# One inference step of a hybrid encoder on one core: the recurrence's normalisers are transposed on chip and stored as whole rows

## The chip, the cores and the metric

The kernel runs on one core of one Trainium2 chip. The metric is the device time of one execution in microseconds (us). Of the kernel before, three runs were timed: 778.81, 780.55 and 783.39 us, median 780.55.

## The reference, cut to what matters

One layer of an encoder is computed for a prompt (1 sequence of 1024 tokens) and for a decode step (8 sequences of 16 new tokens each, so 128 rows as well), all in float32. A normed input of width 1024 goes through one projection, whose columns feed three groups of heads; their gated outputs are joined and go through a second projection.

```python
z = jnp.einsum('bsd,de->bse', rms_norm(x, g_norm), w_in)
# A: 4 heads of differential attention over the new keys, for decode also over 1024 cached ones
# B: 4 heads of an mLSTM, a matrix memory C [64, 64] with a normaliser n [64] for each head
# M: 4 heads of cross-attention into 256 memory tokens
y = x + jnp.einsum('bse,ed->bsd', jnp.concatenate([oa, hb, om], -1), w_out)
```

What matters here is the state of group B. Each chunk of tokens updates it, and the last state is an output, beside `y`, the new keys and values, and others:

```python
C = decay[..., None, None] * C0 + jnp.einsum('bhs,bhsd,bhse->bhde', wS, k, v)
n = decay[..., None] * n0 + jnp.einsum('bhs,bhsd->bhd', wS, k)
```

`C` has the shape [sequence, head, 64, 64] and `n` has [sequence, head, 64]: 4 heads for the prompt, 8 x 4 for the decode step.

## The kernel before, in words

The 1152 rows are cut into 9 tiles of 128 tokens: tiles 0 to 7 are the prompt, tile 8 is the decode step (`DEC`). The normed tiles lie transposed on chip, each split into a high and a low part (`hth`, `htl`), and the weights are split likewise (`wh`, `wl`). A projection of one tile on 512 columns is therefore 24 matmuls of 128 x 512 into one bank of PSUM (`ps_z` or `ps_y`): 8 blocks of the contraction, 3 products each. All matmuls are recorded at line 95, in the helper `mm`.

The work goes through phases: the four heads of A, the gates G, the group M, then two head pairs of B (phases B0 and B1), then the output projection in two halves of columns (O0 and O1). In every phase a weight block is loaded and the tiles pass through it one after the other. `feed` traces the projection of a tile and then one stage more of each tile that is still in the pipeline, so that a tile's later stages lie beside the next tiles' projections. In B0 and B1 a tile of B has three stages: `mlstm_in` (copies out of the bank, two transposes at lines 996 and 997), `mlstm_scores` (loads `mb`, line 1009), and the read-out with the update of the state, which ends in `mlstm_out` (the store of `hb`, line 1042). In phase B0 the decode tile goes first, in B1 third.

Beside B0 and B1 runs the decode attention over the caches, cut into steps by a table: for each of the 8 sequences four loads of keys (`kc`, line 843) and four of values (`vc`, line 875), 512 KB each, in a ring of seven buffers. In O0 the decode attention over the memories follows (`mkc`, line 925, and `mvc`, line 929), two `mkc` buffers; and `out_prep` loads each joined tile (`omx`, line 1136) from a scratch tensor in HBM (`mixd`) for the output projection.

The order in which instructions stand on each engine is not that of the text: a scheduler in the language sets it, by priorities (`ahead`) and by a simulated timeline of its own. All DMAs are issued by SyncE (SP), in one queue and in order; a DMA that must wait for a semaphore holds the ones behind it.

The state of a head pair lies on chip with the head and the row `d` on the 128 partitions. For a decode pair it is `C0` [128, 8 sequences, 65], whose last column is `n`; for the prompt it is `csn` [128, 130], where each head has 65 columns and the last of each 65 is `n`. `C0` has one buffer, so the load of the second pair's state (line 1046) waits until the stores of the first have landed. The stores before: the decode state, 64 columns, at line 1078, and its normaliser, 1 column, at line 1079, once for each pair; the prompt state of each head after the last tile at line 1118 and its normaliser at line 1119. A column that is stored in this way is written as one piece of 4 bytes for each partition and sequence: 1024 pieces for a decode pair, 64 for a prompt head.

Of the kernel before, what the change touches and what calls it, by code (L numbers as in the profile page):

```python
# [11 lines left out]
F32 = mybir.dt.float32  # L12
# [7 lines left out]
P = 128  # L20
# [3 lines left out]
NPT = 8  # L24
# [8 lines left out]
# columns of the relaid w_in: a head of A: q k v ga; ib fb gb; qm gm; a head pair of B: q k v ob  # L33
W_A, W_G, W_M, W_B = 0, 2048, 2312, 2824

# the phases of the projections: priority of the stages before a tile, of its weights and of its
# products; order of the passes for the first tile and the others; banks; engines of the weights' hi
# parts (even k, odd k); k whose lo part is made by Pool; engine that evacuates transposes
# [15 lines left out]
# steps of the decode attention after each tile of the head pairs of B  # L54
# [4 lines left out]
def hymba_step(ctx: ExitStack, tc: tile.TileContext, a: dict, o: dict):  # L59
# [47 lines left out]
    def bc(ap, n):  # L107
        """[p, ...] -> [p, ..., n], repeated along a new last axis"""
        return ap.unsqueeze(len(ap.shape)).broadcast_to(list(ap.shape) + [n])

    def rep(ap, n):
        """[p, ...] -> [p, n, ...], repeated along a new first free axis"""
        return ap.unsqueeze(1).broadcast_to([ap.shape[0], n] + list(ap.shape[1:]))
# [4 lines left out]
    def flat(ap):  # L118
        return ap.rearrange("p a b -> p (a b)")

    # ------------------------------------------------------------------ constants
# [13 lines left out]
    def rsqrt(dst, ss, n):  # L135
        """dst = (ss + n eps) ** -0.5, the reciprocal rms over sqrt(n); the gains carry sqrt(n)"""
        V.tensor_scalar(ss, ss, n * EPS, None, ALU.add)  # L137
        root(dst, ss)
# [15 lines left out]
    # mixed branch outputs and gates of a token tile, stabilisers, values of the new decode tokens  # L154
# [6 lines left out]
    def small_loads():  # L161
# [3 lines left out]
        # carried here: the roots of n, the halves of silu and sigmoid (written with tanh), and, in  # L165
        # the gain of q, 8 * 0.125 / slope of the next head
# [12 lines left out]
    def selectors():  # L179
        # e16[r, q] = (r % 16 == q); bm[r, b] = (r // 16 == b); par[r, i] = ((r // 16) % 2 == i)  # L180
        # h32[r, h] = (r // 32 == h); selc[r, (h, q)] = h32[r, h] * e16[r, q]
# [5 lines left out]
        # sgn[r] = 1 on the rows of map 0, -lam on those of map 1, rows (h, m, q)  # L187
# [6 lines left out]
    def split_T(src, hi, lo, n):  # L194
        """transpose n [128,128] column blocks of src, split into hi and lo [128, n, 128]"""
# [7 lines left out]
    # the tensor engine's clock rises while the first loads run  # L203
# [9 lines left out]
    def weights(w, c0, n, gain=None, spare=()):  # L213
        """columns c0 to c0 + n of a [1024, .] weight, as hi and lo k-tiles; gain scales its rows.
        spare: (pool, tag, bufs) for raw tiles, where there is room"""
# [67 lines left out]
    def norm_T(xt, xp, hi, lo, xT=None):  # L283
        """rms-normed rows (gain not yet applied), transposed and split"""
# [16 lines left out]
    # a token tile's projection is traced ahead of the later stages of the tiles before it  # L301
# [20 lines left out]
    # -------------------------------------------- memory keys and values  # L322
# [9 lines left out]
    # -------------------------------------------- differential attention, prompt  # L332
# [4 lines left out]
    def a_norm(z):  # L337
        """q and k of a head, both maps, over their rms (gains not yet applied)"""
# [16 lines left out]
    def a_post_dec(h, z):  # L355
        """decode tile: q into block-diagonal (m, d) x (b, m, q) stationaries, k transposed"""
# [22 lines left out]
    def a_post(h, t, z, grp):  # L379
        # dist is scaled by the slope, so the scores carry scale / slope  # L380
# [24 lines left out]
        # contraction over (hi, lo) of q in the first map, (lo, hi) in the second  # L405
# [11 lines left out]
    def a_unit(h, t, grp):  # L417
        """attention of one query tile, in two stages"""
# [29 lines left out]
        # the norm takes out the sum of the first map, but for its eps  # L448
# [23 lines left out]
    # -------------------------------------------- mLSTM gate rows: (tile, head) x token in tile  # L472
    R = 36

    def gate_rows():
        # in buffers of the next phase
# [16 lines left out]
        # decode rows restart at every batch  # L493
# [5 lines left out]
        tp = bank("tp")  # L499
# [6 lines left out]
        # log_sigmoid(f) = min(f, 0) - log1p(exp(-|f|)), log1p(u) = 2 atanh(u / (2 + u))  # L506
# [27 lines left out]
        # running stabiliser over the prompt chunks, per head  # L534
# [48 lines left out]
    # -------------------------------------------- cross-attention into the memory  # L583
    def mem_q(z, gt):
        """reciprocal rms of the queries, gate"""
# [10 lines left out]
    def mem_dec_q(z):  # L596
        """decode tile: queries, transposed"""
# [10 lines left out]
    def mem_unit(t, z):  # L608
        # the scores are scaled by the reciprocal rms of q in the softmax; the keys carry q's gain
# [8 lines left out]
        # (hi, lo) of the even heads, (lo, hi) of the odd ones  # L618
# [44 lines left out]
        # this part of the mixed tile stays transposed  # L663
# [43 lines left out]
    # memory keys and values, in buffers that the attention uses later  # L707
    def mem_stages(t):
        def run(z):
# [9 lines left out]
            # 8 of gqm for the 8 that the reciprocal rms of q lacks, times 0.125 of the softmax: none left  # L719
# [63 lines left out]
    # the input and forget gates and gb, behind the last head  # L783
# [27 lines left out]
    # -------------------------------------------- attention over the caches, decode  # L811
    NKD = 1040

    def dec_attention():
# [18 lines left out]
        def scores(b):  # L833
            """rows (h, m, q): exp of the scores over the 1040 keys, signed reciprocal sums"""
# [24 lines left out]
        def values(b, se, sm):  # L859
# [29 lines left out]
            # the two maps, weighted and subtracted: rows (h, q)  # L889
# [21 lines left out]
    # -------------------------------------------- attention over the memories, decode  # L911
    def mem_decode(md):
        """two batches at a time, rows (head, batch of the pair, query)"""
        # contraction over (batch of the pair, head dimension): block-diagonal stationaries
# [48 lines left out]
    # -------------------------------------------- mLSTM  # L963
    # masks over (s, t): prompt causal; decode causal within a batch
# [14 lines left out]
    def mlstm_in(bw, nb, bufs, t, pr, z):  # L979
        """operands of a head pair: values and weighted keys; q (zero-padded), k, gated q transposed"""  # L980
# [24 lines left out]
    def mlstm_scores(bw, nb, t, pr, mask, qk, qp):  # L1005
        """at[s, h, t] = (k_s . q_t) exp(a_s - M_t) on allowed pairs"""
# [11 lines left out]
    def mlstm_out(bw, nb, t, pr, nm, carried, dst, gate):  # L1018
        """read-out, head norm, gates"""
# [13 lines left out]
        # the norm takes out the denominator, but for its eps  # L1033
# [8 lines left out]
        SY.dma_start(out=dst, in_=flat(hb))  # L1042

    def mlstm_decode(pr, z, bufs):
# [24 lines left out]
        for c in range(0, NB, 4):  # L1069
# [9 lines left out]
        SY.dma_start(  # L1079
            out=o["s_n"][0, :, hs].rearrange("b h (d o) -> (h d) b o", o=1), in_=C0[:, :, 64:65]  # L1080
        )
# [3 lines left out]
    def b_stages(pr, t, i_):  # L1085
        def run(z):
# [17 lines left out]
            # state update  # L1104
# [3 lines left out]
            for h2 in range(2):  # L1108
# [7 lines left out]
                if t == NPT - 1:  # L1116
                    h = 2 * pr + h2
                    SY.dma_start(out=o["p_C"][0, 0, h], in_=csn[sl, h2 * 65:h2 * 65 + 64])
                    SY.dma_start(
                        out=o["p_n"][0, 0, h].rearrange("(d o) -> d o", o=1),  # L1120
                        in_=csn[sl, h2 * 65 + 64:h2 * 65 + 65],
                    )
# [5 lines left out]
    def out_prep(t):  # L1128
        """mixed rows, gated (those of the decode tile here), transposed and split over the normed inputs"""
# [37 lines left out]
    # -------------------------------------------- the phases after the last head of A  # L1167
    enter("M")
    ws = weights(a["w_in"], W_M, 512, gnorm)
    for t in [DEC] + list(range(NPT)):  # L1170
        feed(ws, 512, hth[t], htl[t], m_stages(t))
        if t == 0:
            # A is through
# [133 lines left out]
```

## Time and profile before

| | before |
|---|---|
| median of 3 runs | 780.55 us (778.81 to 783.39) |
| span of the profiled execution | 774.3 us |
| the profiled execution's own time beside the span | not on the page; the median of the runs lies 6.25 us above the span |
| TensorE busy | 738.2 us (95%) |
| VectorE, ScalarE, GpSimd busy | 473.7, 333.4, 237.4 us |
| DMA | 106.19 MB in 84387 packets, 16054 of them under 512 bytes |
| B0 begins, O1 ends | about 450 us, 773 us |

The profile is of one execution. Its span runs from the first to the last instruction. TensorE's busy time is the sum of the stretches in which at least one matmul was under way, so that a busy share near 100% does not mean that every matmul ran at its full speed; the clock that the chip granted to TensorE stands beside the stretches. A wait is put down to what released it last. The chain is the work that ended last, followed back from the end: a transfer that stands in it, with a start and a length, is one that the chain could not have ended sooner without.

### The profile page before, as it was taken

What the parts mean: (1) busy time and instruction counts of PE and PEld (TensorE: products, weight loads), DVE (VectorE), ACT (ScalarE), POOL (GpSimd) and SP (SyncE); (2) the same over time, 40 slices, a digit from 0 to 9 for tenths busy, and PEclk for the clock granted to TensorE, in tenths of its full rate; (3) what the DMA queues carried; (4) which work ended last, traced back from release to release, by engine and by line L of the source; (5) the groups of instructions that cost most, each with busy time, mean ns of one, the idle gap of its engine ahead of it and who ended that gap; (6) DMA issues with size and microseconds to landing.
All of it is one profiled execution on the core that took longest, in us unless ns stands there. A gap on an engine that the chain in (4) does not pass through costs nothing.

```text
span 774.3 us, 14523 instructions
## 1 busy us (share of the span) xinstructions
PE 738.2 (95%) x4976; PEld 599.9 (77%) x4976; DVE 473.7 (61%) x1466; ACT 333.4 (43%) x976; POOL 237.4 (31%) x332
## 2 busy tenths in 40 slices
PE   7998999999999999999999999899979997799998
PEld 6776788878888888998878776577747775578887
DVE  6788886677787778677575835347335347644111
ACT  6566634564664466555356532234223334200200
POOL 6653441323223223336313502111012036221500
PEclk9999999999999999999999999999989999999999
DMA  8733430151014112324002407979994728874422
GB/s 310 287 107 109 149 89 22 41 157 45 25 49 124 46 35 70 106 76 124 25 15 46 123 14 251 200 276 327 348 207 157 286 42 299 194 260 124 142 83 95
DMA packets 84387, 106.19 MB, mean 137 GB/s; under 512 B 16054, under 2 KB 52698, under 8 KB 84314
## 3 DMA queue, kind: packets, MB, share of 16 engines
q1 hardware_dynamic: 84314, 105.28, 44.2%
q8 instruction: 39, 0.64, 0.3%
q14 instruction: 34, 0.28, 0.1%
HBM read 86.01 MB, written 19.23 MB: 136 GB/s over the span
## 4 chain that ended last, share of the span: by engine, by line
PE 75%; DMA 9%; DVE 9%; issue 2%; ACT 2%; POOL 2%; SPq 0%; POOLq 0%; DVEq 0%; ACTq 0%
PE ps_z L95 39%; PE ps_y L95 15%; PE ps_s L95 9%; PE ps_av L95 5%; DMA kc<-in_kT_dram 4%; PE ps_tp L459 2%; DVE wl L238 2%; DMA mkc<-in_mkT_dram 1%; DMA wraw<-in_w_in_dram 1%; DMA bgt<-gated 1%; PE ps_tp L200 1%; PE ps_tp L867 1%; PE ps_tp L404 1%; DVE xT L294 1%; POOL asm L133 1%
## 5 line engine op out<-in xcount | busy, mean ns | idle before, releaser
L95 PE MATMUL ps_z<-wh,htl 128*128 128x512 f32 (+2 forms) x552 | 214.8, 391 | 0.1
L95 PE MATMUL ps_z<-wh,hth 128*128 128x512 f32 (+2 forms) x552 | 200.2, 394 | 4.4 <-ACT hth L280 2.1
L95 PE MATMUL ps_z<-wl,hth 128*128 128x512 f32 (+2 forms) x552 | 192.1, 387 | 0.0
L95 PEld LDWEIGHTS ps_z<-wh,hth 128*128 128x128 f32 x552 | 103.6, 190 | 25.5 <-ACT hth L280 2.4
L95 PEld LDWEIGHTS ps_z<-wh,htl 128*128 128x128 f32 x552 | 104.7, 190 | 18.9 <-DVE htl L281 0.8
L95 PEld LDWEIGHTS ps_z<-wl,hth 128*128 128x128 f32 x552 | 103.1, 189 | 18.6 <-issue 1.2
L95 PE MATMUL ps_y<-wh,htl 128*128 128x512 f32 (+2 forms) x176 | 65.6, 374 | 0.0
L95 PE MATMUL ps_y<-wh,hth 128*128 128x512 f32 (+2 forms) x176 | 62.9, 378 | 0.3 <-ACT oa L892 0.3
L133 POOL TENSOR_TENSOR asm<-asm,nhalf 128x4 f32<-128x4 f32 x36 | 39.6, 1100 | 74.4 <-DVE asm L137 58.8
L443 ACT ACTIVATE usx<-usx,usm 128x1024 f32<-128x1024 f32 (+7 forms) x64 | 49.7, 778 | 29.0 <-DVE usm L437 26.5
L95 PE MATMUL ps_y<-wl,hth 128*128 128x512 f32 (+2 forms) x176 | 61.3, 378 | 0.0
L238 DVE SCALAR_TENSOR_TENSOR wl<-wraw,gnm,wh 128x512 fp32r<-128x512 f32 (+1 forms) x62 | 47.0, 783 | 4.6 <-ACT wh L231 3.2
L231 ACT ACTIVATE wh<-wraw,gnm 128x512 fp32r<-128x512 f32 (+1 forms) x56 | 38.0, 706 | 18.2 <-DMA wraw<-in_w_in_dram 15.7
L95 PE MATMUL ps_s<-aqk 128*128 128x256 f32 (+1 forms) x160 | 42.0, 288 | 0.9 <-ACT aqk L412 0.9
L437 DVE CUSTOM_DVE_ANT_0 usx<-ps_s,tab 128x512 f32<-128x512 f32 (+3 forms) x64 | 37.0, 587 | 8.9 <-PE ps_s L95 7.5
L133 POOL TENSOR_TENSOR usm<-usm,nhalf 128x1 f32<-128x1 f32 x32 | 19.6, 612 | 72.3 <-DVE usm L467 67.9
L95 PE MATMUL ps_s<-akl,aqk 128*128 128x256 f32 (+1 forms) x160 | 41.0, 283 | 0.0
L95 PE MATMUL ps_av<-avg,wth 128*128 128x128 f32 x288 | 38.7, 276 | 0.2 <-DVE uot L469 0.2
L95 PEld LDWEIGHTS ps_av<-avg,wth 128*128 128x128 f32 x288 | 36.9, 191 | 2.5 <-ACT wth L460 0.6
L95 PEld LDWEIGHTS ps_y<-wh,hth 128*128 128x128 f32 x176 | 32.8, 188 | 5.8 <-ACT oa L892 0.6
L95 PEld LDWEIGHTS ps_y<-wl,hth 128*128 128x128 f32 x176 | 32.9, 188 | 5.5 <-DVE wl L238 0.3
L95 PEld LDWEIGHTS ps_y<-wh,htl 128*128 128x128 f32 x176 | 33.1, 188 | 5.0
(443 smaller groups left out, 1376.7 us busy)
## 6 DMA issues: line engine op xcount, KB each, us to landing
kc<-in_kT_dram SPq DMA_DIRECT2D x32, 512.0 KB, 8.9
vc<-in_cache_attn_v_dram SPq DMA_DIRECT2D x32, 512.0 KB, 6.8
wraw<-in_w_in_dram SPq DMA_DIRECT2D x56, 256.0 KB, 3.0
omx<-mixd SPq DMA_DIRECT2D x9, 512.0 KB, 4.1
out_dram<-oxt SPq DMA_DIRECT2D x17, 256.0 KB, 4.3
xt<-in_x_prompt_dram SPq DMA_DIRECT2D x8, 512.0 KB, 7.7
wraw<-in_w_out_dram SPq DMA_DIRECT2D x16, 256.0 KB, 4.2
oxt<-in_x_prompt_dram SPq DMA_DIRECT2D x16, 256.0 KB, 3.4
```

The source lines that it names most:

```text
L95: PE.matmul(out, lhsT, rhs, start=start, stop=stop)
L133: G.tensor_tensor(dst, ss, nhalf[:, 0:ss.shape[1]], ALU.pow)
L200: PE.transpose(tv[:, i, :], src[:, (c + i) * P:(c + i + 1) * P], ident)
L231: S.activation(wh[:, 0:n], raw[:, 0:n], AF.Copy, scale=g_)
L238: V.scalar_tensor_tensor(wl[:, 0:n], raw[:, 0:n], g_, f(wh[:, 0:n]), ALU.mult, ALU.subtract)
L294: V.scalar_tensor_tensor(xT[:, cs], xT[:, cs], math.sqrt(D), rep(rb, 4), ALU.mult, ALU.mult)
L404: PE.transpose(tp[:, i], flat(nd[:, 2 * i:2 * i + 2]), ident)
L437: V.tensor_tensor_reduce(s_[:, c * 512:c * 512 + w], sp[:, 0:w], tab[:, tx:tx + w], -slope, BIG if c == 0 else sm[:, m:m + 1], ALU.add, AL ...
L443: S.activation(s_[:, 0:nk], s_[:, 0:nk], AF.Exp, bias=last, scale=-1.0, accum_out=sm[:, 4 + m:5 + m])
L459: PE.transpose(tp[:, i], sx[0][:, (c + i) * P:(c + i + 1) * P], ident)
L867: PE.transpose(tp[0:pn, c - c0, :], se[:, c * P:c * P + pn], ident)
```

## The change

The normalisers are no longer stored as columns. A new function, `store_n`, transposes them on TensorE (8 columns, one for each sequence, for a decode pair; 2 columns, one for each head, for a prompt pair), copies the result from PSUM to a tile `nt` on ScalarE, and stores rows: for a decode pair 8 rows of 128 elements with one DMA, for a prompt pair one row of 64 elements for each of the two heads. The transposes take a bank from the ring `tp`, which the other transposes share. All else in the diff is comments that were dropped (not shown).

```diff
+    def store_n(dst, cols, diag=False):
+
+        n = cols.shape[1]
+        tp = bank("tp")
+        PE.transpose(tp[0:n, 0:P], cols, ident)
+        nt = bw.tile([8, P], F32, tag="nt", name="nt", bufs=1)
+        S.copy(nt[0:n], tp[0:n, 0:P])
+        if diag:
+            for h2 in range(2):
+                SY.dma_start(out=dst[h2:h2 + 1], in_=nt[h2:h2 + 1, h2 * 64:h2 * 64 + 64])
+        else:
+            SY.dma_start(out=dst, in_=nt[0:n])
+
...
         SY.dma_start(out=o["s_C"][0, :, hs].rearrange("b h d e -> (h d) b e"), in_=C0[:, :, 0:64])
-        SY.dma_start(
-            out=o["s_n"][0, :, hs].rearrange("b h (d o) -> (h d) b o", o=1), in_=C0[:, :, 64:65]
-        )
+        store_n(o["s_n"][0, :, hs].rearrange("b h d -> b (h d)"), C0[:, :, 64])
...
                     SY.dma_start(out=o["p_C"][0, 0, h], in_=csn[sl, h2 * 65:h2 * 65 + 64])
-                    SY.dma_start(
-                        out=o["p_n"][0, 0, h].rearrange("(d o) -> d o", o=1),
-                        in_=csn[sl, h2 * 65 + 64:h2 * 65 + 65],
-                    )
+            if t == NPT - 1:
+                hs = slice(2 * pr, 2 * pr + 2)
+                store_n(o["p_n"][0, 0, hs], csn[:, 64::65], True)
             cst[pr] = csn
```

In the changed kernel the lines behind `store_n` stand 13 further down up to the prompt's stores and 10 further down from there on; the transpose is line 1048, the copy 1050, the stores 1053 (prompt) and 1055 (decode).

Since the scheduler places the instructions, the change moves others too. On SP's queue in phase B0, where the first decode pair's state is stored (`out_dram<-C`), with - for before and + for the change:

```order
-L1078 DMA out_dram<-C_5586 128x8x64
-L1079 DMA out_dram<-C_5586 128x8x1
-L843 DMA kc<-in_kT_dram 128x1024
+L1091 DMA out_dram<-C_5586 128x8x64
 L1042 DMA mixd_79<-hb 128x128
 L991 DMA bgt<-gated_91 128x128
-L843 DMA kc<-in_kT_dram 128x1024 x2
-L1009 DMA mb<-mtd 128x256
-L1046 DMA C_7191<-in_Cn_dram 128x520
+L1055 DMA out_dram<-nt 8x128
+L1059 DMA C_7199<-in_Cn_dram 128x520
+L875 DMA vc<-in_cache_attn_v_dram 128x2x512
```

The load of the second pair's state (`C<-in_Cn_dram`) has moved ahead of the first batch's last value load, which stood before the state store, and ahead of three key loads, which follow in the next row.

On TensorE in phase B0 before, where the updates of the decode state (`ps_av<-vx,km`) end and the scores of the first cached keys (`ps_s<-kc,qz`) stand:

```order
L95 MATMUL ps_s<-vx_5346,mb 128x65 x2
L95 MATMUL ps_s<-qn_5354,qk 128x256
L95 MATMUL ps_av<-vx_5340,km 64x65 x8
L95 MATMUL ps_s<-kc,qz 32x256 x16
L95 MATMUL ps_z<-wh,hth_123 128x512
L95 MATMUL ps_z<-wh,htl_132 128x512
```

On TensorE in the changed kernel, where the same scores stand now, within the projection of tile 5 (`hth_124`, `htl_133`):

```order
L996 MATMUL ps_tp<-ident,kg 128x128
L997 MATMUL ps_tp<-ident,bqn 128x128
L95 MATMUL ps_z<-wh,htl_133 128x512
L95 MATMUL ps_z<-wh,hth_124 128x512
L95 MATMUL ps_s<-qn_5354,qk 128x256
L95 MATMUL ps_s<-kc,qz 32x256 x8
L95 MATMUL ps_av<-vx_5340,kw 64x65 x2
```

Between the last update and the scores there now stand 39 matmuls of the projections of tiles 4 and 5, and among them the new transpose (line 1048); the scores of the next batch follow after 9 more instead of 37.

On SP's queue in phase B1, where the second decode pair's state is stored:

```order
-L1078 DMA out_dram<-C_7191 128x8x64
-L1079 DMA out_dram<-C_7191 128x8x1
+L1091 DMA out_dram<-C_7199 128x8x64
 L1042 DMA mixd_87<-hb 128x128
 L991 DMA bgt<-gated_92 128x128
 L909 DMA mixd_87<-oa 16x4x128 x8
+L1055 DMA out_dram<-nt 8x128
 L1042 DMA mixd_81<-hb 128x128
 L991 DMA bgt<-gated_93 128x128
```

The normaliser's store has moved behind the eight stores of the decode attention's output (`oa`), directly ahead of the next tile's `hb` and `bgt`.

## Rows read from the trace of the kernel before

**Rows 1.** The page's first part: busy us, share of the span, instructions.
```profile
PE 738.2 (95%) x4976; PEld 599.9 (77%) x4976; DVE 473.7 (61%) x1466; ACT 333.4 (43%) x976; POOL 237.4 (31%) x332
```

**Rows 2.** TensorE's waits, 440 to 774 us: waiter, releaser: us, times, longest.
```profile
PE ps_s L95 <- DMA kc<-in_kT_dram: 7.0, 3, 3.2
PE ps_s L95 <- DMA mkc<-in_mkT_dram: 3.9, 1, 3.9
PE ps_s L95 <- DVE mb L1015: 2.2, 1, 2.2
...
PE ps_s L95 <- issue: 1.3, 1, 1.3
PE ps_s L95 <- DVE bns L1026: 1.2, 1, 1.2
```

**Rows 3.** The chain of waits from 430 us on: start, length in us, what.
```profile
481.75 13.02 DMA kc<-in_kT_dram
...
563.68 10.54 DMA kc<-in_kT_dram
...
630.71 8.44 DMA bgt<-gated
...
665.83 10.80 DMA mkc<-in_mkT_dram
```

**Rows 4.** Stores of the normalisers: duration of an issue in ns, first and last start.
```profile
L1079 SPq DMA_DIRECT2D out_dram<-C x2: 574/1318/2063, 479.6 to 626.6; - x2
...
L1119 SPq DMA_DIRECT2D out_dram<-cs x4: 473/540/588, 560.2 to 661.3; - x4
```

**Rows 5.** DMA issues: count, KB each, median us to landing; key loads' landing alone.
```profile
mkc<-in_mkT_dram SPq DMA_DIRECT2D x4, 512.0 KB, 4.9
...
out_dram<-cs SPq DMA_DIRECT2D x4, 0.2 KB, 12.7
out_dram<-C SPq DMA_DIRECT2D x2, 4.0 KB, 10.8
...
DMA to landing us min/median/max: 3.7/8.9/11.1
```

**Rows 6.** Stretches: length, busy PE, PEld, DVE, ACT, POOL; clock, DMA share, GB/s.
```profile
482.00:495.00 13.00, 10.30 (x67) 7.81 (x69) 3.80 (x15) 3.77 (x12) 1.84 (x3) 1.00 0.96 147
495.42:498.83 3.41, 3.41 (x34) 2.46 (x34) 1.01 (x6) 0.00 (x0) 0.73 (x1) 0.50 1.02 345
...
540.00:560.00 20.00, 20.00 (x196) 15.49 (x195) 7.81 (x32) 4.50 (x14) 1.43 (x2) 1.00 0.96 352
...
561.00:574.20 13.20, 8.82 (x124) 5.13 (x122) 3.60 (x18) 3.90 (x17) 3.56 (x6) 0.99 0.84 114
573.92:580.75 6.83, 6.49 (x19) 3.47 (x19) 3.29 (x11) 1.00 (x5) 0.00 (x0) 0.50 1.07 401
...
676.32:679.74 3.42, 2.97 (x16) 2.10 (x17) 1.71 (x6) 0.00 (x0) 1.32 (x3) 0.50 1.00 379
```

**Rows 7.** TensorE in order of time: start, us, what, [idle before <- releaser].
```profile
494.90 0.64 PE L95 MATMUL ps_s<-kc,qz 128*32 128x256 f32 x8 [2.70 <-DMA kc<-in_kT_dram]
...
574.26 1.06 PE L95 MATMUL ps_s<-kc,qz 128*32 128x256 f32 x2 [3.19 <-DMA kc<-in_kT_dram]
...
676.77 1.08 PE L95 MATMUL ps_s<-mkc,qzm 128*32 128x256 f32 x8 [3.94 <-DMA mkc<-in_mkT_dram]
```

**Rows 8.** DMA queue, 626 to 630.7 us: packets, MB, share of 16 engines.
```profile
q1 hardware_dynamic: 2286, 0.45, 47.9%
```

**Rows 9.** One transpose on TensorE, one small copy on ScalarE: ns min/median/max.
```profile
L996 PE MATMUL ps_tp<-ident,kg x18: 272/328/421, 453.7 to 656.9; 128*128 128x128 f32 x18
...
L78 ACT COPY qn<-ps_tp x18: 261/261/264, 454.9 to 660.5; 64x128 f32<-64x128 f32 x18
```

**Rows 10.** SP in order of time around 702 us: the `dom` stores, then `omx`.
```profile
701.89 2.65 SPq L961 DMA_DIRECT2D mixd<-dom  x4
...
705.76 0.34 SPq L1136 DMA_DIRECT2D omx<-mixd  x1
```

## The prediction

> **What bounds the kernel now.** I read the page first, then TensorE's waits in the second half of the span, then the chain of waits, then the stretches around what these named. TensorE is busy for 738.2 us of the 774.3 us span [rows 1]; what can still be won is its idle time and the time in which it runs at half clock. From 440 us on its longest waits are for key loads (`kc`, 7.0 us in three waits), for a memory-key load (`mkc`, 3.9), for `mb` (2.2), one of 1.3 put down to "issue", which stands among the products of the same key loads, and one for `bns` (1.2) [rows 2]. The chain names four transfers that it stood behind for 8 to 13 us each [rows 3]. The reader is to see what stands just ahead of all four: the two stores of the decode normalisers are issued at 479.6 and 626.6 us, the four of the prompt's between 560.2 and 661.3 us [rows 4], and the long transfers are issued at 481.75, 563.68, 630.71 and 665.83 us. So there are four places.
>
> These stores are tiny (4.0 KB and 0.2 KB), but land 10.8 and 12.7 us after their issue [rows 5]. What follows them crawls: from 482 to 495 us the DMA engines are 96% busy and move 147 GB/s, while from 540 to 560 us, equally 96% busy, they move 352; from 561 to 574.2 us they move 114 [rows 6]. [...]
>
> TensorE pays twice. It stands still for 2.70 us until 494.90, for 3.19 until 574.26 and for 3.94 until 676.77 [rows 7]; and right after each of the three the granted clock is 0.50 of full speed, its 1.2 GHz level, for 3.41, 6.83 and 3.42 us, of which it was busy 3.41, 6.49 and 2.97 [rows 6]. At the other level that work takes half, so the clock costs 1.71 + 3.25 + 1.49 = 6.4 us.
>
> **The change part by part.** Removed: 2 stores of 1024 pieces of 4 bytes and 4 of 64. Added: 4 transposes on TensorE, 4 copies on ScalarE, 2 stores of eight 512-byte rows, 4 of one 256-byte row. Moved: much of what follows the first decode tile of B, since the scheduler orders anew.
>
> *First place (479.6).* To be recovered: 2.70 of waiting, 1.71 of clock, and the wait of 1.1 at 479 that is left of the 7.0 [rows 2, 7] after 2.70 and 3.19, since the scores of the first batch now come 39 products of the projection later: 5.5. New waits come with the order. The projection of tile 4 now starts right behind the last product that reads the value tile which two ScalarE copies must first refill and drain: two copies of 0.26 [rows 9] and two hand-overs, an estimate of 0.8. The scores of the second batch now stand close behind those of the first, with the transposes of its exponentials between them, and only 9 projection products as cover: an estimate of 1.2. On SP's queue the load of the next states has moved ahead of a value load and three key loads, and there it waits until the state store (256-byte pieces) has landed; all of them are late if that is late. I take 5.5 - 2.0 = 3.5. Upper end 5.5. Lower end: if the state store needs the 10.8 us of the old normaliser store, the loads start at 490 and, at 8.9 us for a key load [rows 5], land at 499, where TensorE wants them near 494: 5 us of waiting, 1.7 of clock, the 2.0 above, against 5.5: -3.
>
> *Second place (560.2 to 561.5).* To be recovered: 1.25 + 3.19 + 3.25 = 7.7. The key load was issued at 563.68; without two issues of 0.6 ahead of it, at 562.4. Little else was under way there (114 GB/s), so I reckon with the shortest landing of a key load, 3.7 us [rows 5]: 566, before TensorE comes to it, which was at 574.26 - 3.19 = 571.1 and without the wait of 1.25 will be at 569.8. I leave 1.2 for the two `mb` loads in front: 6.5. Lower end, with 8.9 us: landing at 571.3, a wait of 1.5, and the clock as it was: 4.4 - 1.5 = 3.
>
> *Third place (626.6).* To be recovered: 2.21 + 1.25 = 3.5 [rows 2]. The `bgt` load took 8.44 us [rows 3]. But now the transpose stands on TensorE ahead of the next tiles' transposes, behind 20 projection products, and the row store stands on SP between the eight stores of the decode attention and the next tiles' `hb` and `bgt`: if the copy is late, these wait. I take 2.0, from 0 to 3.5.
>
> *Fourth place (658.5 to 661.3).* To be recovered: 3.94 + 1.49 = 5.4 [rows 6, 7]. TensorE arrived at 676.77 - 3.94 = 672.8; a memory-key load that takes its median of 4.9 us [rows 5] instead of 10.80 lands at 665.83 + 4.9 = 670.7. The new transpose stands behind most of this. I take 4.6, from 1.5 to 5.4.
>
> *Costs.* A full 128x128 transpose takes 0.33 us [rows 9]; four: 1.3 at most, I take 1.0. The ScalarE copies (0.26) lie beside TensorE's work. What is late next: from 540 to 560 us TensorE has no idle time and the DMA engines are 96% busy [rows 6]; a TensorE that comes there some us sooner finds loads that are not there yet. I take off 2.0 (an estimate, from 0 to 4).
>
> Sum: 3.5 + 6.5 + 2.0 + 4.6 - 1.0 - 2.0 = 13.6 us off the span of 774.3, so 760.7. The page gives no time for its own execution beside the span; the median of the runs, 780.55, lies 6.25 above it, and with that the forecast is 766.9. Its ends: all recovered and nothing lost, 22.1 - 1.0 = 21.1, 759.5; all four at their lower ends with the costs at their highest, 1.5 - 5.3 = -3.8, 784.4. All four at the low end at once is the rivals' affair; the likeliest case by itself spans 760 to 772.
>
> **A rule against it.** From 626 to 630.7 us 2286 packets, most of them the pieces of 4 and of 256 bytes, took 47.9% of 16 engines, 16 ns a piece [rows 8]; so the 1024 pieces cost the engines about 1 us themselves. The Trainium skill ("DMA: Bandwidth & Descriptors", Why small descriptors are slow (HBM only)) puts the cost of a small piece at a few bus cycles and 32 bytes of descriptor; by that alone the change would save some 2 us of engine time and none on the path. The piece's own time agrees with this; what the rule doesn't have is the wait of those behind.
>
> **Rivals.**
> *The keys are late because the queue is full (no change).* For it: the busy share of 0.8 to 0.96 [rows 6], and that a key load takes 8.9 us even at its median. Against it: 147 and 114 GB/s in those stretches. Then only the engines' 2 us go, off the path, and the transposes come on top: -1.0 of cost, 780 to 782, say 780.9.
>
> *The 256-byte pieces share the blame (half).* The state stores stay: 1024 pieces of 256 bytes beside each decode store, 64 beside each prompt one. For it: they are always issued together with the 4-byte ones. Against it: the four `dom` stores, 512 such pieces, were issued from 701.89 on and had landed by 705.76, when the load that reads them was issued [rows 10]. If half of each stall stays: 16.6 / 2 - 1.0 - 1.0 = 6.3, 774.3. The Trainium skill (the same page, Specifications) says that below 512 bytes the engine reads, modifies and writes, which would put both sizes in one class; the `dom` row says otherwise.
>
> *The state load holds the keys (slower).* If it is the state stores alone that hold the memory up, nothing is won at the four places, and the new order makes the first one worse: the load of the next states waits on SP for the state store, with a value load and three key loads behind it. By the lower end above that costs 3 us, the transposes 1.3, and the row store ahead of `hb` and `bgt` at the third place about 0.5: 780.55 + 4.8 = 785.4. It decides from the point where the state store lands later than about 490 us, 11 after its issue; under that the keys are there when they are wanted.
>
> **How the numbers follow.** Forecast 0.66, half 0.16, no change 0.09, slower 0.09. What a measurement of this kernel can tell from no change is about 0.5%, 3.9 us, so faster means under 776.65: 0.66 + 0.16 = 0.82; same 0.09; slower 0.09. The range from 759 to 777 holds nearly all of the first case and the half one, and leaves out the rest, just under 2 in 10.
>
> **What would show it.** Right: no packet stream under 150 GB/s at a busy share over 0.8 behind the four stores; the chain no longer names a `kc`, `bgt` or `mkc` transfer of 8 us or more behind them; the granted clock stays at 1.00 from 480 to 700 us; the five waits of [rows 2], 15.6 us in sum, fall to under 6. The first place is the weakest step: there I expect short waits in other places, behind the state load and the exponentials. Wrong: if waits of 8 us and more stay behind the state stores, or if the clock still falls near 495, or if the time gained by 580 us is gone by 700.

## The result and the profile after

The changed kernel takes 760.27 us (758.75 to 761.60, 4 runs), 0.9735 of the kernel before, with a 95% interval of 0.9702 to 0.9767. Timed a second time it was 0.978 (0.9757 to 0.9804). The forecast was 766.9, with a range of 759 to 777. The kernel before had medians from 776.5 to 782 in the comparisons below; so kernels are compared by their ratio to the runs of it that stood beside them.

The busy line answers to [rows 1]: TensorE is busy for about as long as before, in a span of 757.8 us instead of 774.3.

```profile
PE 733.4 (97%) x4980; PEld 596.4 (79%) x4980; DVE 475.1 (63%) x1466; ACT 333.9 (44%) x980; POOL 234.4 (31%) x332
```

TensorE's waits of the changed kernel from 455 us on (waiter, releaser: us, times, longest) answer to [rows 2]. Of the 15.6 us that stood there for `kc`, `mkc`, `mb`, "issue" and `bns`, the view still lists the 0.5 for `kc` in the last row shown; the longest wait that is left is 1.2.

```profile
PE ps_av L95 <- DVE cs L1124: 1.2, 1, 1.2
PE ps_s L95 <- DVE esm L850: 1.0, 2, 0.6
PE ps_z L95 <- ACT bth L993: 0.7, 2, 0.5
...
PE ps_tp L867 <- ACT se L854: 0.6, 2, 0.3
PE ps_s L95 <- DMA kc<-in_kT_dram: 0.5, 2, 0.4
```

The chain of waits of the changed kernel from 430 us on (start, length, what) answers to [rows 3]. It still names two key loads of 8 us and more, but neither stands close behind a store of a normaliser (those start at 483.6, 569.2, 627.7 and 668.1 us), and TensorE waits 0.5 us for key loads in all.

```profile
520.14 9.46 DMA kc<-in_kT_dram
...
591.72 8.26 DMA kc<-in_kT_dram
```

The transfers behind the new stores do not crawl. Two stretches of the changed kernel that begin with the store of the first place and the first store of the second (length, then busy PE, PEld, DVE, ACT and POOL with their instructions, then granted clock, DMA share, GB/s) answer to the 147 and 114 GB/s of [rows 6]:

```profile
483.60:496.60 13.00, 12.12 (x97) 8.39 (x96) 5.95 (x23) 3.83 (x13) 1.94 (x4) 1.00 0.59 180
569.20:582.40 13.20, 13.20 (x77) 10.19 (x76) 5.86 (x23) 4.29 (x16) 2.66 (x4) 1.00 0.69 259
```

Behind the stores of the third and fourth place it is 269 and 229 GB/s, and from 480 to 700 us the clock is 1.00. So every sign that the prediction had named for being right is there.

To see where the time was won, I cut both spans at events that both have: the first transposes at line 996, then the first product of `vn,ewt` of the fifth, sixth and eighth sequence, then the last update of a state in B. The first, second, fourth and fifth stretch hold the four places in their order. The kernel before (stretch: length, busy PE with its instructions, ..., granted clock, DMA share, GB/s):

```profile
453.70:564.86 111.16, 107.40 (x1031) 78.30 (x1030) 54.88 (x197) 33.66 (x111) 15.87 (x26) 0.98 0.81 248
564.86:594.65 29.79, 25.35 (x198) 16.97 (x194) 10.80 (x39) 7.46 (x27) 5.39 (x8) 0.89 0.59 170
594.65:622.80 28.15, 27.80 (x336) 19.67 (x332) 12.08 (x45) 8.23 (x25) 4.08 (x7) 1.00 0.73 259
622.80:653.20 30.40, 25.93 (x175) 19.95 (x171) 17.34 (x65) 13.53 (x48) 14.44 (x19) 1.00 0.53 159
653.20:774.30 121.10, 112.34 (x676) 90.41 (x675) 43.71 (x110) 12.01 (x32) 26.92 (x32) 0.99 0.51 158
```

The changed kernel, the same stretches:

```profile
455.50:564.30 108.80, 106.34 (x1032) 76.27 (x1031) 54.34 (x197) 33.96 (x112) 15.10 (x27) 1.00 0.75 254
564.30:586.49 22.19, 22.19 (x198) 15.77 (x195) 10.79 (x39) 7.59 (x28) 5.05 (x8) 1.00 0.64 221
586.49:615.26 28.77, 28.06 (x336) 19.60 (x333) 11.79 (x45) 8.34 (x25) 4.06 (x7) 1.00 0.76 254
615.26:641.77 26.51, 25.04 (x175) 19.86 (x171) 16.21 (x57) 12.67 (x45) 14.09 (x20) 1.00 0.60 197
641.77:757.80 116.03, 112.06 (x679) 89.91 (x678) 46.18 (x117) 12.85 (x38) 27.25 (x31) 1.00 0.49 162
```

The counts of TensorE's instructions agree to within 3, so the lengths may be compared: 2.4, 7.6, -0.6, 3.9 and 5.1 us were won, 18.3 in all; 1.8 were lost ahead of 455.5 us, where nothing was changed. TensorE's idle time in these stretches fell from 21.8 to 8.6 us, which is 13.2; the other 5.1 are busy time that became shorter. In sum that is what the clock explains: it is 1.00 in every stretch, where [rows 6] had three falls to 0.50, which had cost 6.4; the new transposes (four of 0.27) give 1.1 of it back, which leaves 5.3. Stretch by stretch it agrees less well: the busy time fell by 1.1, 3.2, -0.3, 0.9 and 0.3 us, and the fourth stretch, whose clock was 1.00 before too, has no fall to explain its 0.9. What made that part shorter stays open.

### The profile page after: what moved, and what is told of

Its sections match the earlier page's. It is cut to its first block, busy times and chain, and to the rows that moved or that the text cites. A ratio compares the mean times of both kernels' runs of the same rounds, so it can differ in the third digit from the quotient of the medians.

```text
span 757.8 us, 14555 instructions
## 1 busy us (share of the span) xinstructions
PE 733.4 (97%) x4980; PEld 596.4 (79%) x4980; DVE 475.1 (63%) x1466; ACT 333.9 (44%) x980; POOL 234.4 (31%) x332
## 4 chain that ended last, share of the span: by engine, by line
PE 77%; DVE 8%; DMA 7%; issue 2%; ACT 2%; POOL 2%; SPq 1%; DVEq 0%; POOLq 0%; ACTq 0%
PE ps_z L95 40%; PE ps_y L95 15%; PE ps_s L95 9%; PE ps_av L95 5%; DMA kc<-in_kT_dram 2%; PE ps_tp L459 2%; DMA wraw<-in_w_in_dram 2%; PE ps_tp L867 1%; DMA oxt<-in_x_prompt_dram 1%; PE ps_tp L404 1%; DVE wl L238 1%; DVE xT L294 1%; PE ps_tp L200 1%; DMA bgt<-gated 1%; POOL asm L133 1%
## 5 line engine op out<-in xcount | busy, mean ns | idle before, releaser
L95 PE MATMUL ps_z<-wh,htl 128*128 128x512 f32 (+2 forms) x552 | 212.5, 386 | 0.3 <-DVE htl L192 0.3
```

Of the source, the lines that this page charges most:

```text
L95: PE.matmul(out, lhsT, rhs, start=start, stop=stop)
```

## The experiments

Twelve kernels were run. Those that take something away from the kernel before or the changed one say what they leave out in their expectation.

**Old order, rows.** Diff to the kernel before:

```diff
-        SY.dma_start(
-            out=o["s_n"][0, :, hs].rearrange("b h (d o) -> (h d) b o", o=1), in_=C0[:, :, 64:65]
-        )
+        SY.dma_start(out=o["s_n"][0, :, hs].rearrange("b h d -> b (h d)"), in_=flat(C0)[0:8, 392:520])
...
-                    SY.dma_start(
-                        out=o["p_n"][0, 0, h].rearrange("(d o) -> d o", o=1),
-                        in_=csn[sl, h2 * 65 + 64:h2 * 65 + 65],
-                    )
+                    SY.dma_start(out=o["p_n"][0, 0, h:h + 1], in_=csn[h2 * 64:h2 * 64 + 1, h2 * 65:h2 * 65 + 64])
```

> The kernel before, with its order up to the fourth place, but each normaliser store writes whole rows (8 of 512 bytes, or one of 256) from rows of the state tile itself: the transposing is left out, so the stored normalisers are other numbers. If the 4-byte pieces are the cause: the waits behind all four places go, some 762 us (between 758 and 767). If the gain came from the new order of instructions: this kernel keeps the old order and stays at 777 to 782.

Measured: 756.52 us, ratio 0.9697 (0.9656 to 0.9738). The gain doesn't come from the new order. The old one with rows looks even faster than the changed kernel; the intervals overlap here, and the repeat on one chip, below, sets them apart.

**Pieces apart.** The 4-byte pieces stay, and the order on TensorE is that of the kernel before to the last row. The two stores are replaced by:

```diff
+        scr = dpool.tile([P, 8, 64], F32, name=f"scr{pr}")
+        SY.dma_start(out=scr[:, :, 0:1], in_=C0[:, :, 64:65])
...
+                    scp = dpool.tile([64, 64], F32, name=f"scp{h}")
+                    SY.dma_start(out=scp[:, 0:1], in_=csn[sl, h2 * 65 + 64:h2 * 65 + 65])
```

> The kernel before with the same 4-byte pieces, as many and in the same places of every queue, but written 256 bytes apart into a scratch tensor, so that no two of them share a stretch of memory; the normaliser outputs are not written. If the size of a piece is the cause: 780, with kc and mkc transfers of 8 to 13 us behind the stores as before. If it is that neighbouring pieces fall into the same stretch of memory and are written one after the other: about 764.

Measured: 756.36 us, 0.9692 (0.9653 to 0.9731). This overturned the cause as I had it: there are as many 4-byte pieces as before, and the whole stall is gone. The 13.0 and 13.2 us behind the first stores, which answer to the stretches of 147 and 114 GB/s in [rows 6], now read so:

```profile
481.70:494.70 13.00, 13.00 (x82) 9.40 (x81) 5.90 (x24) 4.21 (x14) 2.22 (x4) 1.00 0.89 273
560.00:573.20 13.20, 13.20 (x152) 7.94 (x151) 6.24 (x27) 5.00 (x18) 3.46 (x6) 1.00 0.78 262
```

TensorE has no gap, and the transfers run at 273 and 262 GB/s.

**Pieces packed, same place.** `scr` is [8, 128] and `scp` [64, 1], and both are written from end to end:

```diff
+        scr = dpool.tile([8, P], F32, name=f"scr{pr}")
+        SY.dma_start(out=scr.rearrange("b (x o) -> x b o", o=1), in_=C0[:, :, 64:65])
...
+                    scp = dpool.tile([64, 1], F32, name=f"scp{h}")
+                    SY.dma_start(out=scp, in_=csn[sl, h2 * 65 + 64:h2 * 65 + 65])
```

> The kernel before with its 4-byte pieces as packed as before, but into the same scratch tensors' place as in the run with pieces 256 bytes apart; the normaliser outputs are not written. If the neighbourhood of the pieces is the cause: 777 to 781, landing 10 to 13 us. If it was the output tensor that held them (its place in memory): 756.

Measured: 779.62 us, 1.0034 (1.0006 to 1.0061). So it is not the output tensor. The stores by themselves, first apart (the run before this one), then packed: line, duration of the issue in ns, first and last start, and the time to landing.

```profile
L1080 SPq DMA_DIRECT2D scr<-C x2: 585/1741/2897, 481.0 to 617.6; - x2
...
DMA to landing us min/median/max: 3.1/3.1/3.1
...
L1119 SPq DMA_DIRECT2D scp<-cs x4: 451/552/588, 558.7 to 647.3; - x4
...
DMA to landing us min/median/max: 2.3/2.3/2.3
```

```profile
L1080 SPq DMA_DIRECT2D scr<-C x2: 574/1326/2077, 482.9 to 632.4; - x2
...
DMA to landing us min/median/max: 11.5/11.5/11.5
...
L1119 SPq DMA_DIRECT2D scp<-cs x4: 452/540/588, 565.7 to 666.9; - x4
...
DMA to landing us min/median/max: 12.8/12.8/12.8
```

The same bytes from the same tiles at the same places of the queue land 8.4 and 10.5 us later when they are written side by side.

What a stall is made of shows on SP. Behind the prompt's first two stores it issues, among others, a store of `hb` (start, duration of the issue, what); first with the pieces apart, then packed:

```profile
563.08 0.40 SPq L1042 DMA_DIRECT2D mixd<-hb  x1
```

```profile
570.16 5.74 SPq L1042 DMA_DIRECT2D mixd<-hb  x1
```

Nothing that SP has to issue can start in those 5.74 us (5.46 in the kernel before), and the DMA engines are then nearly idle, with a share of 0.05 and 10 GB/s:

```profile
570.20:575.90 5.70, 4.95 (x54) 2.05 (x42) 0.40 (x3) 0.69 (x2) 0.73 (x1) 1.00 0.05 10
```

The third place shows the same: the eight `oa` stores behind the second decode pair take 7.8 to 8.3 us to issue in all six kernels whose decode pairs are packed, that before among them, and 3.6 to 3.8 in the eight others. So a stall is not everywhere a stretch of busy engines, although the shares of [rows 6] suggest it. What holds SP and the transfers these views do not show.

**How far apart.** Small stores were added in the quiet stretches of A:

```diff
...
+            w = 2 ** t
+            sc = dpool.tile([64, w], F32, name="apart_" + "abcdefgh"[t])
+            SY.dma_start(out=sc[:, 0:1], in_=ot[0:64, 0:1])
...
+            sc = dpool.tile([64, w], F32, name="wide_" + "abcdefgh"[t])
+            SY.dma_start(out=sc, in_=ot[0:64, 0:w])
```

> The kernel before with 24 small stores added in the quiet stretches of heads 1 to 3 of A, each from a column of a tile that is stored there anyway into a scratch tensor of its own: 64 pieces of 4 bytes at 4, 8, 16, ... 512 bytes from one another (apart_a to apart_h); 4, 8, ... 128 packed pieces, 1024 packed ones in the layout of a decode pair, and 1024 at 256 bytes (count_a to count_h); 64 packed pieces of 4, 8, ... 512 bytes (wide_a to wide_h). What is read is the time from issue to landing. If pieces that share a stretch of memory wait for each other, and that stretch is some 64 bytes: 12.7 us at 4 bytes, halving with each doubling of the distance, 2.3 from 64 bytes on; by count, (12.7 - 2.3) / 16 = 0.65 us a piece: 4.9 us for 4, 7.5 for 8, and 12.7 for 16 and for every larger number; by width, falling to 2.3 at 64 bytes. If all pieces of a store wait for each other when packed, 0.16 us each: 3 us for 4 and 23 for 128. If only the size counts: 12.7 at every distance, falling with the width alone.

It was half a miss: the trace has a landing for five of the 24 stores only, 7.3 us for 64 packed pieces, 3.0 at 16 bytes, 1.6 at 32, 1.9 at 256, and 1.9 for 64 packed pieces of 32 bytes. The 3.0 hold an issue that took 1.78 us by itself, where the other stores of the distances took 0.45 to 0.74. The second try loads each store's pieces back, so that SP stands until they have landed:

```diff
...
+                SY.dma_start(out=sc[:, 0:1], in_=ot[0:n, 0:1])
+                SY.dma_start(out=lb[0:n], in_=sc[:, 0:1])
...
```

> As the ladder of small stores (distances apart_a to apart_h, numbers count_a to count_h), without the widths; behind each store a load reads its pieces back, and SP stands before it until the store has landed: start of the load less start of the store is the landing. In the first ladder only some stores had a landing: 7.3 us for 64 packed pieces, 3.0 at 16 bytes, 1.6 at 32, 1.9 at 256. If the pieces that share a stretch of 64 bytes wait for each other: about 4.5 at 8 bytes, and equal times for 16, 32, 64 and 128 packed pieces. If a stretch is 32 bytes, which 16 bytes at 3.0 and 32 at 1.6 would fit as well: equal times from 8 pieces on. If all pieces of a packed store wait for each other: 128 pieces take about twice the time of 64 (13 us), and 1024 far more.

SP in order of time, each store and the load behind it (start, duration of the issue, what): 64 pieces at 32 bytes (d), 16 (c), 8 (b) and 4 (a).

```profile
239.35 0.46 SPq L477 DMA_DIRECT2D apart_d<-uot  x1
...
240.99 0.46 SPq L478 DMA_DIRECT2D lb<-apart_d  x1
...
244.03 1.63 SPq L477 DMA_DIRECT2D apart_c<-uot  x1
...
246.92 0.46 SPq L478 DMA_DIRECT2D lb<-apart_c  x1
...
250.78 0.46 SPq L477 DMA_DIRECT2D apart_b<-uot  x1
254.37 0.46 SPq L478 DMA_DIRECT2D lb<-apart_b  x1
...
258.50 0.46 SPq L477 DMA_DIRECT2D apart_a<-uot  x1
...
265.11 0.46 SPq L478 DMA_DIRECT2D lb<-apart_a  x1
```

From the start of a store to the start of the load behind it: 1.64, 2.89, 3.59 and 6.61 us. From 32 bytes on nothing is lost: it stays at 1.65, 1.66, 1.93 and 1.70 at 64, 128, 256 and 512. At 8 bytes the excess over 1.64 is 1.95 and at 4 it is 4.97. At 16 the 2.89 are an upper bound, since SP itself came late to the load: the issue of the store took 1.63 instead of 0.46, and two other stores stood in between until 246.77. Whether pieces 16 bytes apart disturb each other stays open. So the limit lies between 8 and 32 bytes, not at the 64 that I had assumed. The Trainium skill ("DMA: Bandwidth & Descriptors", How a descriptor splits into AXI transactions) puts one beat of the bus at 32 bytes; the runs neither show nor exclude that this is the limit, and the page says nothing of pieces that share a beat.

The counts bore out none of the three guesses. SP in order of time again, the store and the load behind it for 1024 packed pieces (g), 32 (d), 16 (c) and 8 (b):

```profile
286.98 0.43 SPq L481 DMA_DIRECT2D count_g<-uot  x1
...
297.51 0.34 SPq L482 DMA_DIRECT2D lb<-count_g  x1
...
322.50 0.42 SPq L477 DMA_DIRECT2D count_d<-uot  x1
...
326.93 0.32 SPq L478 DMA_DIRECT2D lb<-count_d  x1
...
330.62 0.49 SPq L477 DMA_DIRECT2D count_c<-uot  x1
...
335.02 0.32 SPq L478 DMA_DIRECT2D lb<-count_c  x1
...
338.70 0.33 SPq L477 DMA_DIRECT2D count_b<-uot  x1
340.13 0.28 SPq L478 DMA_DIRECT2D lb<-count_b  x1
```

From start to start, 4 and 8 packed pieces take 1.5 and 1.4 us and so lose nothing, although the 8 span no more than 32 bytes; 16 and 32 take the same 4.4, 64 take 6.6, 128 take 7.9 and 1024 take 10.5; 1024 pieces at 256 bytes (h) take 3.05. It grows with the number, but far more slowly. Why 8 pieces go free and how 64 pieces reach 12.7 us in the kernel (6.6 to 7.3 here, alone) stays open: which DMA engine wrote which piece these views don't show, and whether it matters wasn't tried.

**One kind of store at a time.** The decode pairs in rows, the prompt's heads in columns:

```diff
...
-                store_n(o["p_n"][0, 0, hs], csn[:, 64::65], True)
+                    SY.dma_start(
+                        out=o["p_n"][0, 0, h].rearrange("(d o) -> d o", o=1),
+                        in_=csn[sl, h2 * 65 + 64:h2 * 65 + 65],
+                    )
```

> The changed kernel, rows for the two decode pairs only; the prompt's four stores are columns of 64 4-byte pieces again. By the sum of the prediction the second and fourth place come back, 6.5 + 4.6 us: 771. If the time depends on the number of 4-byte pieces, the prompt's (256 of 2304) are a ninth of the matter: 762 to 763.

Measured: 775.36 us, 0.9956 (0.9930 to 0.9982): the four stores of 64 pieces cost some 14 to 17 us of the 17 to 21 that the change wins, though they are a ninth of the pieces. That is 3 to 6 us more than the 6.5 and 4.6 of the sum, so both expectations missed. TensorE's two longest gaps (start, length, what, [idle before]) stand behind them, at the second and fourth place, and the clock falls behind both:

```profile
575.80 1.06 PE L95 MATMUL ps_s<-kc,qz 128*32 128x256 f32 x2 [5.82 <-DMA kc<-in_kT_dram]
...
670.71 0.69 PE L200 MATMUL ps_tp<-ident,omx 128*128 128x128 f32 x2 [6.78 <-DVE mwt L947]
...
576.00:583.00 7.00, 7.00 (x32) 3.95 (x31) 3.29 (x13) 1.19 (x4) 0.00 (x0) 0.66 1.05 397
669.00:677.00 8.00, 6.29 (x46) 4.73 (x47) 6.80 (x22) 0.86 (x4) 2.40 (x4) 0.54 0.96 342
```

The other way round, the prompt in rows (`store_n` as in the changed kernel), the decode pairs in columns:

```diff
-        store_n(o["s_n"][0, :, hs].rearrange("b h d -> b (h d)"), C0[:, :, 64])
+        SY.dma_start(
+            out=o["s_n"][0, :, hs].rearrange("b h (d o) -> (h d) b o", o=1), in_=C0[:, :, 64:65]
+        )
```

> The changed kernel, rows for the prompt's heads only; the two decode pairs store columns of 1024 4-byte pieces again. The order stays near that of the kernel before up to the second place. By the sum of the prediction, the first and third place come back, without the new order's 2.0: 760 + 5.5 + 2.0 = 767 to 768. If the prompt's stores were the whole of the matter (the run with decode rows only lost 15 of 21 us): 762.

Measured: 763.36 us, 0.9801 (0.9745 to 0.9858). It lies between the two expectations; its order at the first place is the old one, so that the last experiment below (0.9724, the old order with rows everywhere) is its neighbour: the decode columns cost about 0.77%, 6 us, there, near the 5.5 + 2.0 of the sum; but the two were timed on different chips, and the intervals overlap.

**New order, columns.** The changed kernel's transposes and copies with the stores of before:

```diff
...
-            SY.dma_start(out=dst, in_=nt[0:n])
+            SY.dma_start(out=dst.rearrange("b (x o) -> x b o", o=1), in_=src)
```

> The changed kernel, its four transposes and copies kept (their result is not stored), but the normalisers stored as columns of 4-byte pieces again, each store one or a few rows earlier on SP's queue. If the pieces are the cause: 776 to 783, with half-clock stretches behind the stores. If the new order of instructions made the gain: 760 to 764.

Measured: 789.33 us, 1.0112 (1.0071 to 1.0152), slower than either expectation. The chain of waits from 480 us on (start, length, what), then two of TensorE's longest waits (waiter, releaser: us, times, longest):

```profile
480.27 12.38 DMA out_dram<-C
492.80 2.67 DMA C<-in_Cn_dram
...
638.33 8.53 DMA bgt<-gated
```

```profile
PE ps_av L95 <- DVE cs L1125: 7.6, 1, 7.6
...
PE ps_s L95 <- DVE mb L1015: 3.6, 1, 3.6
```

The column store that the state load has to wait for lands after 12.38 us, and the load is issued at 492.80, 13.6 us after the state store of 479.17. TensorE then waits 3.6 us, but not for keys: it waits for `mb`, which stands on VectorE behind work on the loaded state. The slower rival of the prediction had the load late, as it is, but not this wait: the keys behind the load hold TensorE for 0.6 us. The longest wait, 7.6 us, is at the third place, to which that rival gave about 0.5: the `bgt` load behind the packed store takes 8.53 us, and in this order the update of `cs`, for which TensorE waits, stands on VectorE behind the work on what it loads. In the changed kernel the state load is issued 8.1 us after the state store of 478.80, and no key load is late:

```profile
486.89 0.34 SPq L1059 DMA_DIRECT2D C<-in_Cn_dram  x1
```

**A way by scratch.** The prompt as in the changed kernel, the decode pairs apart into scratch, from there into 8 rows, and out:

```diff
+        scr = dpool.tile([P, 8, 64], F32, name=f"scr{pr}")
+        SY.dma_start(out=scr[:, :, 0:1], in_=C0[:, :, 64:65])
+        nt = bw.tile([8, P, 1], F32, tag="nt", name="nt", bufs=1)
+        SY.dma_start(out=nt, in_=scr[:, :, 0:1].rearrange("x b o -> b x o"))
+        SY.dma_start(out=o["s_n"][0, :, hs].rearrange("b h d -> b (h d)"), in_=nt.rearrange("b x o -> b (x o)"))
```

> A version that should beat both: the prompt's normalisers as in the changed kernel, the decode pairs' written 256 bytes apart into a scratch tensor, loaded from there into 8 rows on chip, and stored as rows; TensorE's order is then that of the kernel before up to 560 us. If the old order is worth the 3.8 us by which the run with rows in the old order beat the changed kernel: 756 to 758. If the transposes or the extra transfers cost them: 760 to 762.

Measured: 762.17 us (757.65 to 763.89), 0.9788 (0.9719 to 0.9857). It doesn't beat the changed kernel, and its interval holds both expectations: inconclusive.

**Another bank.** One word of the changed kernel:

```diff
-        tp = bank("tp")
+        tp = bank("av")
```

> The changed kernel with one word changed: the transposes take their bank from the ring of the updates (av), not from that of the other transposes (tp). The order then stays that of the kernel before at the first place: the scores of the first keys right behind the last update, the key loads ahead of the state load. If the new order costs 3.8 us against the old one: 756.5 to 758. If the 3.8 between the changed kernel and the run with rows in the old order came from the transposes, or from runs on different chips: as the changed kernel beside it.

> The changed kernel once more, to compare with the two beside it on one chip: 760, 0.974 of the kernel before.

> The run with rows from the state tile itself in the old order once more (the transposing left out), on the same chip as the changed kernel: 756 to 757 if its order and the missing transposes are worth 3.8 us; 759 to 760 if that was a difference of chips.

Measured on one chip: other bank 756.56 us, 0.9724 (0.9700 to 0.9748); the changed kernel again 761.28, 0.9780 (0.9757 to 0.9804); rows in the old order again 754.73, 0.9696 (0.9676 to 0.9716). The intervals of the first two don't meet: the bank alone is worth about 0.56%, 4.4 us, and the version with the other bank beats both kernels. Between it and the run without transposes lie 0.28%, 2.2 us, with intervals that overlap: four transposes of 0.27 would be 1.1 of it. The other bank's first stretch shows where its gain is:

```profile
455.60:561.77 106.17, 105.94 (x1030) 77.03 (x1028) 54.82 (x195) 33.99 (x113) 15.36 (x27) 1.00 0.75 260
```

It takes 106.17 us to the second place, the changed kernel 108.80; TensorE is idle there for 0.2 instead of 2.5. The two spans differ by 2.6 us in all (755.2 and 757.8), so the profiles put the gain into this stretch, with the old order of the first place; the rest of the 4.4 they don't show.

## Why the prediction came out as it did

The direction, the four places and the waits behind them were right. The size was short: 13.65 us were forecast, and 21.7 and 16.4 were measured in the two comparisons; 760.27 lies 1.3 us above the lower end of the range. The cause was named too widely, and one term of the sum was not what I took it for.

*First place, 3.5 less part of the costs.* 2.4 measured. The waits that the new order brings were estimated at 0.8 and 1.2; the longest of the waits for `bth`, `esm` and `se` in the changed kernel stand there, 0.5, 0.6 and 0.3. Part of what was to be recovered went into them. With the other bank, the place gives 111.16 - 106.17 = 5.0, near the 5.5 that were there to be recovered.

*Second place, 6.5.* 7.6: nothing was late behind it; the 1.2 held back for the `mb` loads weren't needed.

*Third place, 2.0.* 3.9, a little more than the 3.5 that I took for its upper end. The row store ahead of `hb` and `bgt` held nobody up. TensorE's idle time fell by 3.0, although the wait of 1.2 for `cs` is new there; the other 0.9 is the busy time that stays open.

*Fourth place, 4.6.* 5.1 with the rest of the span.

*Costs, 1.0 and 2.0.* Four transposes of 0.27 are 1.1. The loads that I feared to be late behind 540 us were not: TensorE is busy for 106.34 of 108.80 us up to there.

*The step from the span to the time, 6.25.* This is the term that was mis-sized. Wherever both are listed, the time is 1.7 to 1.9 us above the span (759.53 against 757.8 in the profiled one), but for three executions with 2.3 or 2.4. By that the profiled execution of the kernel before took about 776.1, some 4.5 us less than the median run. So the span was forecast 2.9 too long (760.7 against 757.8) and the time 6.6; the larger part of the miss, 3.7, is this step.

*The cause.* That the stores of 4-byte pieces stand ahead of all four stalls was true and not enough. The same pieces at 256 bytes cost nothing (0.9692), and packed again they cost everything (1.0034). What stalls is a store of many pieces that begin closer together than some distance between 8 and 32 bytes; in the rows no two pieces begin so close. The prediction also took the slow stretches for stretches of busy engines, from shares of 0.96 and 0.84 in [rows 6]. Cut finer, that does not hold at the second place: from 565 to 570.1 us, while SP stands in the issue of `hb`, the share is 0.33 and 6 GB/s are moved. The forecast needed only that the transfers are late, which they are.

*Rivals.* No change by a full queue: out, since with the pieces apart the same transfers run at 273 GB/s. Half by the 256-byte pieces: out, the state stores stayed in every run, and the gain is whole. The state load that holds the keys: in the run with columns in the new order the load is late, 13.6 us after the state store, but by the packed stores, and it is `mb` and not the keys for which TensorE then waits; in the changed kernel it is issued after 8.1 us, under the 11 from which it was to decide. The rule against the change, that a piece costs the engines only its own 16 ns, holds for pieces that lie apart.

## What to carry to other kernels

A column that is stored into consecutive words of HBM is small in every sum of bytes and can still cost 2% of a kernel, through what stands behind it on the queue: look for stretches with few GB/s, whether the DMA engines are busy there or not, for an issue on the queue that takes microseconds, and for the small store just ahead of them. To store it in rows costs one transpose of 0.27 us on TensorE; where the layout is free, pieces 32 bytes apart landed as fast here as any. And where a scheduler orders the work, an added instruction's bank can cost more than the instruction: compare the orders that different rings give (0.9724 against 0.9780 here).

## What was not expected of the hardware

The landing of a store depends more on where its pieces fall than on their number: 1024 pieces of 4 bytes land after 3.1 us when they are 256 bytes apart and after 11.5 side by side. The Trainium skill ("Perfetto Trace Analysis", DMA Instruction — HWDGE (DVE, Sync)) says that a transfer's last step waits for its writes to be confirmed and that this can be surprisingly long towards HBM; the 11.5 us fit that, though no view here splits a landing into its steps, and the run with the pieces apart shows that it need not be long.

In this kernel 64 packed pieces land as late as 1024 do, 12.7 against 10.8 us [rows 5], where alone they take 6.6 against 10.5; and of the two kinds the prompt's four stores cost more than twice as much of the time. Behind packed stores the issuing queue was held too: SP stood for 5.74 us in one issue, with the DMA engines at a share of 0.05.
